# Squares between two feed-forward products: ScalarE's second activation in place of GpSimd's product

## The chip, the cores and the metric

The kernel runs on one core of a Trainium2 chip. The metric is the device time of one execution in microseconds (us); the time before is a median over three runs. The core has five engines that take instructions in the order in which they stand: TensorE (PE in the profile; its weight loads have a row of their own, PEld), VectorE (DVE), ScalarE (ACT), GpSimd (POOL) and SyncE (SP), which here issues nearly all DMAs.

## The reference, cut to what matters

A sequence of 1024 frames of 1024 channels runs through two layers. Each has a token mixer (RWKV-7 in the first layer, an S5 state-space layer with a gated projection in the second) and then a feed-forward block; a layer norm follows every one of the four. The change lies in the feed-forward block alone:

```
def sq_relu_mlp(x, w1, w2):
    return jnp.square(jax.nn.relu(x @ w1)) @ w2

h = layer_norm(DN_ALPHA * h + sq_relu_mlp(h, mlp_w1[i], mlp_w2[i]), ln_g[2*i+1], ln_b[2*i+1])
```

`w1` is 1024 x 4096 and `w2` 4096 x 1024, all in float32. The square of the rectified value stands between the two products.

## The kernel before

Channels lie on the 128 partitions and frames along a row. The frames are taken in two halves of 512, so a tile is 128 x 512: half A (`hA`, operands `oAh`, `oAl`) and half B (`hB`, `oBh`, `oBl`).

**Products in three parts.** A float32 operand is split into a high part of TensorE's own float32 kind and a remainder: `split` has ScalarE cast the high part (L152) and VectorE subtract it (L153). A product is then three matmuls (L198): high by high, high by low, low by high. Weights go the same way: SyncE brings 128 x 512 of them into `wraw`, ScalarE casts `whi`, VectorE makes `wlo`. `wraw` has two buffers, `whi` and `wlo` three each.

**A feed-forward block.** `blocks` gives two functions. `up(b)` makes two tiles of 128 hidden channels: 24 matmuls into a PSUM tile `d` (three buffers for the whole kernel), ScalarE's Relu of it into `rl` (L986), the square in place (L987), and the split into `qbuf` (L152, L153). `down(b)` multiplies these two tiles with `w2`, in eight groups of six matmuls, and VectorE adds each PSUM result into `hA` or `hB` (L1003). `up(b+1)` stands ahead of `down(b)`, so that a block's squares are wanted only a block later.

**Both halves at once.** In the second layer twelve of the sixteen blocks are done for both halves together by `both`, with seven half-size products (L1040) in place of eight. There `power` does Relu (L1046), square (L1047) and split, four times a block, into `qh` and `ql`.

Squares are 128 in all: 80 of L987 and 48 of L1047.

**What sets the order.** The code does not fix the order of the instructions. A scheduler puts them on the engines, by priorities that the kernel sets with `rank(...)`, by the buffers that are free, and by its own idea of what each instruction costs. So another engine or cost at one place can move the instructions around it on every engine.

**Where the blocks lie.** The first layer's blocks for half A run beside the last chunks of the RWKV recurrence (about 760 to 1005 us), beside the layer norm of half B and the building of the S5 tables (`s5_tables`, a chain of VectorE products, L1266 to L1268, with small TensorE products `pk` and `pb`; about 1040 to 1270 us). Those of half B run beside the layer norm and the S5 layer of half A (products L1310, L1317, L1331, L1383, L1391) and then alone, to about 1675 us. The second layer's blocks run from about 1950 us to the end.

**A layer norm** takes a sum (L870 to L876), `pm` (L878), subtraction (L880), squares on ScalarE (L884, L887), their sum on VectorE and GpSimd (L888), `pq` (L892), a power on GpSimd (L895), `pr` (L900), a product (L903) and scale and shift on ScalarE (L904).

Of the kernel before, what the change touches and what calls it, by code (L numbers as in the profile page):

```python
# [10 lines left out]
AF = mybir.ActivationFunctionType  # L11
# [61 lines left out]
def trunk(ctx, tc, A):  # L73
    nc = tc.nc
    V, S, G, PE, SP = nc.vector, nc.scalar, nc.gpsimd, nc.tensor, nc.sync
# [75 lines left out]
    def split(src, hi, lo, e=None):  # L151
        S.copy(hi, src)  # L152
        (e or V).tensor_sub(lo, src, hi.bitcast(F32))  # L153
# [12 lines left out]
    def wload(src, kt, n, key=None):  # L166

        step = 512 // n
        out = []
        for k0 in range(0, kt, step):  # L170
            kept = low.get((key, k0)) if key else None
            raw = wp.tile([128, step, n], F32, tag="wraw", name="wraw", bufs=2)
            SP.dma_start(raw, src[:, k0 : k0 + step])
            hi = wp.tile([128, step, n], F32R, tag="whi", name="whi")
            lo = wp.tile([128, step, n], F32R, tag="wlo", name="wlo")
            nw[0] += 1
            if kept is not None:
                SP.dma_start(lo.bitcast(F32).rearrange("p k n -> p (k n)"), kept)
                S.copy(hi, raw)
            else:  # L180
                split(raw, hi, lo, G if nw[0] % WLG[0] in WLG[1] and WLG[2] <= nw[0] < WLG[3] else V)
                if key:
                    low[key, k0] = dr.tile([128, 512], F32, name=f"low{len(low)}")
                    SP.dma_start(low[key, k0], lo.bitcast(F32).rearrange("p k n -> p (k n)"))
            out += [(hi[:, k], lo[:, k]) for k in range(step)]
        return out
# [35 lines left out]
    def dense(p, w, xs):  # L222
        n = len(xs)
        for k in range(n):
            mm3(p, w[k][0], w[k][1], xs[k][0], xs[k][1], k == 0, k == n - 1)
# [11 lines left out]
    def psd():  # L237
        return pd.tile([128, HT], F32, tag="d", name="d")
# [736 lines left out]
    def blocks(i, h, xo, qbuf):  # L975

        nw = 512 // KB2
        qs = {}

        def up(b):  # L980
            qs[b] = []
            for n in range(KB2):
                p = psd()
                dense(p, wload(A["mw1"][i, b * KB2 + n], KT, 128), xo)
                r = tp.tile([128, HT], F32, tag="ev", name="rl", bufs=EVB)
                S.activation(r, p, AF.Relu)  # L986
                G.tensor_mul(r, r, r)  # L987
                qt = qbuf[:, n + KB2 * (b % 2)]
                split(r, qt[:, 0], qt[:, 1])
                qs[b].append((qt[:, 0], qt[:, 1]))  # L990

        def down(b, first=False, cs=slice(0, HT)):
            for n2 in range(C // nw):
                w = wload(A["mw2"][i, b, n2], KB2, nw)
                for n in range(nw // 128):
                    p = psd()[:, cs]
                    dense(p, [(x[:, n * 128 : (n + 1) * 128], y[:, n * 128 : (n + 1) * 128]) for x, y in w],
                          [(x[:, cs], y[:, cs]) for x, y in qs[b]])
                    z = h[n2 * (nw // 128) + n][:, cs]
                    if first:  # L1000
                        V.scalar_tensor_tensor(z, z, ALPHA, p, op0=ALU.mult, op1=ALU.add)
                    else:
                        V.tensor_add(z, z, p)  # L1003

        return up, down

    def mlp(i, h, xo, qbuf):
# [10 lines left out]
    def both(i, hP, hQ, P, Q, tops, first):  # L1018

        nw = 512 // KB2  # L1020
        P1, P2, Q2 = P[0:4], P[4:8], Q[4:8]
        T1, T2, T3, T4 = tops
        qs = {}

        def raw(pool, tag, f, k0):
            t = pool.tile([128, 4, 128], F32, tag=tag, name="raw", bufs=2)
            SP.dma_start(t, A["mw1"][i, f][:, k0 : k0 + 4])
            return t

        def weights(t):  # L1030
            hi = wp.tile([128, 4, 128], F32R, tag="whi", name="whi")
            lo = wp.tile([128, 4, 128], F32R, tag="wlo", name="wlo")
            split(t, hi, lo)
            return hi, lo

        def product(p, t, xs, add=False):
            hi, lo = weights(t)
            for k in range(4):
                for j, (w, x) in enumerate(((hi, xs[k][0]), (hi, xs[k][1]), (lo, xs[k][0]))):
                    PE.matmul(p, w[:, k], x, start=not add and k + j == 0, stop=k == 3 and j == 2, skip_group_check=True)  # L1040

        def ev(name):
            return tp.tile([128, HT], F32, tag="ev", name=name, bufs=EVB)

        def power(dst, x):
            S.activation(dst, x, AF.Relu)  # L1046
            G.tensor_mul(dst, dst, dst)  # L1047
            qh, ql = (jp.tile([128, HT], F32R, tag=nm, name=nm, bufs=6) for nm in ("qh", "ql"))
            split(dst, qh, ql)
            return qh, ql  # L1050

        def up(b):
            f1, f2 = 2 * b, 2 * b + 1
            r11, r12 = raw(wp, "wraw", f1, 0), raw(wp, "wraw", f1, 4)
            r21, r22 = raw(tp, "la", f2, 0), raw(tp, "la", f2, 4)
            s1, s2 = (tp.tile([128, 4, 128], F32, tag="m", name=nm, bufs=2) for nm in ("s1", "s2"))
            G.tensor_add(s1, r21, r22)
            G.tensor_sub(s2, s1, r11)
            pa_ = psd()
            product(pa_, r11, P1)  # L1060
            m1 = ev("m1")
            S.copy(m1, pa_)
            pb_ = psd()
            product(pb_, s2, T2)
            V.tensor_add(m1, pb_, m1)
            product(pa_, r12, P2, True)
            r = ev("rl")
            c1 = power(r, pa_)
            G.tensor_sub(r21, r11, r21)
            pc_ = psd()  # L1070
            product(pc_, r21, T3)
            u3 = ev("u3")
            V.tensor_add(u3, pc_, m1)
            pd_ = psd()
            product(pd_, s1, T1)
            m5 = ev("m5")
            S.copy(m5, pd_)
            G.tensor_sub(s2, r12, s2)
            pe_ = psd()
            product(pe_, r22, T4)  # L1080
            G.tensor_add(m5, m5, u3)
            V.tensor_sub(u3, u3, pe_)
            product(pd_, s2, Q2, True)
            V.tensor_add(m1, pd_, m1)
            c2, c4, c3 = power(u3, u3), power(m5, m5), power(m1, m1)
            qs[b] = (c1, c2), (c3, c4)

        def down(b):
            for n2 in range(C // nw):
                w = wload(A["mw2"][i, b, n2], KB2, nw)  # L1090
                for n in range(nw // 128):
                    for h, q, fresh in ((hP, qs[b][0], b == first), (hQ, qs[b][1], False)):
                        p = psd()
                        dense(p, [(x[:, n * 128 : (n + 1) * 128], y[:, n * 128 : (n + 1) * 128]) for x, y in w], q)
                        z = h[n2 * (nw // 128) + n]
                        if fresh:
                            V.scalar_tensor_tensor(z, z, ALPHA, p, op0=ALU.mult, op1=ALU.add)
                        else:
                            V.tensor_add(z, z, p)

        return up, down
# [491 lines left out]
```

## Time and profile before

| | |
|---|---|
| time, median of 3 runs | 2673.59 us (2672.07 to 2679.01) |
| the profiled execution, its own time | 2674.25 us |
| its span, first to last instruction | 2672.5 us |
| mean granted TensorE clock | 0.960 |
| busy: PE, DVE, ACT, POOL | 2495.2, 1846.4, 1133.2, 629.8 us |
| L987, 80 squares on POOL | 90.8 us |
| L1047, 48 squares on POOL | 53.02 us |

A group's row in the profile has the line, the engine, the operation, what it writes and reads, the shapes and the count, then the busy time, the mean duration of one in ns, and the idle time of the engine just before these instructions with what ended it. A row of a table by stretches has each engine's busy time in the stretch with the number of its instructions, the granted TensorE clock (1.00 is full), the share of the DMA engines' time and what they moved. A row of waits names the waiting instruction, what ended the wait, the sum, the number and the longest.

### The profile page before, as it was taken

How to read it: one execution, taken by the hardware profiler on the slowest of the kernel's cores; microseconds unless marked ns; L12 is line 12 of the kernel's file. 1: busy time of each engine (PE TensorE's matmuls, PEld its weight loads, DVE VectorE, ACT ScalarE, POOL GpSimd, SP SyncE). 2: the span in 40 equal slices, each digit the busy share in tenths (PEclk: the TensorE clock that was granted, in tenths of full speed). 3: DMA queues.
4: the chain of work that ended last, by engine and by line, in shares of the span. 5: the costliest groups of instructions: out<-in, count | busy, mean ns of one | idle time of the engine just before them, and what ended most of it. 6: DMA issues, size and time to landing. Idle time of an engine off the chain costs nothing.

```text
span 2672.5 us, 43745 instructions
## 1 busy us (share of the span) xinstructions
PE 2495.2 (93%) x16624; PEld 2022.1 (76%) x16624; DVE 1846.4 (69%) x3271; ACT 1133.2 (42%) x2028; POOL 629.8 (24%) x532
## 2 busy tenths in 40 slices
PE   7899979989889999888899999998999999999996
PEld 5678757788667777766777888886777888888875
DVE  7367677487896868799785555775587656565576
ACT  7555665554444334245433333433453322323234
POOL 3121542342442222011100011200233313223111
PEclk9999889998889999999999999998999999999998
DMA  4765455663323324456465333264222111111133
GB/s 152 243 217 182 155 166 178 206 183 126 97 74 92 93 93 141 132 155 154 148 224 179 99 95 96 90 210 143 91 83 79 56 51 52 52 51 52 52 103 99
DMA packets 213074, 330.31 MB, mean 124 GB/s; under 512 B 20736, under 2 KB 85376, under 8 KB 212864
## 3 DMA queue, kind: packets, MB, share of 16 engines
q1 hardware_dynamic: 212864, 327.52, 39.3%
q8 instruction: 131, 2.15, 0.3%
q14 instruction: 79, 0.65, 0.1%
HBM read 260.28 MB, written 67.16 MB: 123 GB/s over the span
## 4 chain that ended last, share of the span: by engine, by line
PE 54%; DVE 11%; DMA 4%; issue 2%; ACT 1%; SPq 1%; POOL 1%; ACTq 0%; DVEq 0%; POOLq 0%
PE d L198 40%; PE d L1040 9%; DVE wlo L153 2%; DMA wraw<-in_mw_dram 2%; DMA yl<-s_y 1%; PE pu L1317 1%; DVE hA L1003 1%; PE pbu L1331 1%; DVE qbuf L153 0%; DVE hA L880 0%; ACT whi L152 0%; PE py L1383 0%; DMA s_y<-yg 0%; DVE tw L1267 0%; DVE ca L1266 0%
## 5 line engine op out<-in xcount | busy, mean ns | idle before, releaser
L152 ACT CAST whi<-wraw 128x512 fp32r<-128x512 f32 x524 | 324.3, 619 | 748.5 <-PE d L198 430.3
L153 DVE TENSOR_TENSOR wlo<-wraw,whi 128x512 fp32r<-128x512 f32 x524 | 409.1, 782 | 271.9 <-ACT whi L152 266.0
L198 PE MATMUL d<-qbuf,whi 128*128 128x512 f32 (+1 forms) x1344 | 414.5, 391 | 21.4 <-DVE hA L1003 13.7
L198 PE MATMUL d<-oAh,whi 128*128 128x512 f32 (+1 forms) x768 | 310.8, 412 | 14.2 <-ACT ev L428 9.3
L198 PE MATMUL d<-oAh,wlo 128*128 128x512 f32 (+1 forms) x768 | 309.4, 409 | 9.7 <-DVE wlo L153 6.3
L198 PE MATMUL d<-oAl,whi 128*128 128x512 f32 (+1 forms) x768 | 306.7, 403 | 8.2 <-DVE oAl L153 8.2
L198 PEld LDWEIGHTS d<-qbuf,whi 128*128 128x128 f32 x1344 | 248.5, 192 | 80.2 <-DVE hA L1003 15.8
L198 PE MATMUL d<-qbuf,wlo 128*128 128x512 f32 (+1 forms) x672 | 259.3, 388 | 6.5 <-DVE wlo L153 6.3
L987 POOL TENSOR_TENSOR rl<-rl 128x512 f32<-128x512 f32 x80 | 90.8, 1136 | 704.2 <-ACT rl L986 677.9
L198 PE MATMUL d<-oBh,whi 128*128 128x512 f32 x512 | 204.0, 400 | 13.5 <-ACT whi L152 10.4
L198 PE MATMUL d<-oBh,wlo 128*128 128x512 f32 x512 | 203.7, 399 | 8.1 <-DVE wlo L153 8.1
L198 PE MATMUL d<-oBl,whi 128*128 128x512 f32 x512 | 202.5, 396 | 0.0
L198 PEld LDWEIGHTS d<-oAh,whi 128*128 128x128 f32 (+1 forms) x768 | 147.3, 194 | 49.2 <-ACT ev L428 11.6
L198 PEld LDWEIGHTS d<-oAh,wlo 128*128 128x128 f32 (+1 forms) x768 | 147.2, 193 | 44.9 <-DVE wlo L153 8.5
L198 PEld LDWEIGHTS d<-oAl,whi 128*128 128x128 f32 (+1 forms) x768 | 147.8, 194 | 39.3 <-DVE oAl L153 10.1
L198 PEld LDWEIGHTS d<-qbuf,wlo 128*128 128x128 f32 x672 | 128.1, 191 | 35.0 <-DVE wlo L153 9.4
L198 PE MATMUL d<-qh,wlo 128*128 128x512 f32 x384 | 151.4, 394 | 0.0
L198 PE MATMUL d<-ql,whi 128*128 128x512 f32 x384 | 150.6, 392 | 0.0
L198 PE MATMUL d<-qh,whi 128*128 128x512 f32 x384 | 149.3, 389 | 0.0
L198 PEld LDWEIGHTS d<-oBh,whi 128*128 128x128 f32 x512 | 97.3, 191 | 37.8 <-ACT whi L152 12.4
L1003 DVE TENSOR_TENSOR hB<-hB,d 128x512 f32<-128x512 f32 (+1 forms) x168 | 104.4, 632 | 30.6 <-PE d L198 28.8
L198 PEld LDWEIGHTS d<-oBh,wlo 128*128 128x128 f32 x512 | 97.4, 190 | 31.7 <-DVE wlo L153 10.0
(455 smaller groups left out, 5175.1 us busy)
## 6 DMA issues: line engine op xcount, KB each, us to landing
wraw<-in_mw_dram SPq DMA_DIRECT2D x376, 256.0 KB, 2.7
wraw<-in_glu_dram SPq DMA_DIRECT2D x64, 256.0 KB, 2.7
low<-wlo SPq DMA_DIRECT2D x52, 256.0 KB, 2.8
wlo<-low SPq DMA_DIRECT2D x52, 256.0 KB, 3.8
raw<-in_mw_dram SPq DMA_DIRECT2D x48, 256.0 KB, 2.6
wraw<-in_wk_dram SPq DMA_DIRECT2D x32, 256.0 KB, 3.4
wraw<-in_wr_dram SPq DMA_DIRECT2D x32, 256.0 KB, 4.0
wraw<-in_wv_dram SPq DMA_DIRECT2D x32, 256.0 KB, 4.4
```

Source lines behind the costliest of these rows:

```text
L152: S.copy(hi, src)
L153: (e or V).tensor_sub(lo, src, hi.bitcast(F32))
L198: bulk.append((PE.matmul(p, w, x, **kw).ins, x.shape[-1]))
L987: G.tensor_mul(r, r, r)
L1003: V.tensor_add(z, z, p)
L1040: PE.matmul(p, w[:, k], x, start=not add and k + j == 0, stop=k == 3 and j == 2, skip_group_check=True)
L1317: PE.matmul(p[64 * (1 - e) : 64 * (1 - e) + 64, g], u1[:, j, g].rearrange("p s c -> p (s c)"), sel[:, e], start=True, stop=True)
L1331: PE.matmul(p[qs, ri, g2], tb[:, g2, ri, qs], u[:, 2 * g2 + par], start=True, stop=True)
```

## The change

Both squares are taken by ScalarE's Square activation in place of GpSimd's product of the tile with itself. What is computed, and the tiles it goes through, stay the same.

```
@@ up, in blocks
                 S.activation(r, p, AF.Relu)
-                G.tensor_mul(r, r, r)
+                S.activation(r, r, AF.Square)
                 qt = qbuf[:, n + KB2 * (b % 2)]
                 split(r, qt[:, 0], qt[:, 1])
@@ power, in both
             S.activation(dst, x, AF.Relu)
-            G.tensor_mul(dst, dst, dst)
+            S.activation(dst, dst, AF.Square)
             qh, ql = (jp.tile([128, HT], F32R, tag=nm, name=nm, bufs=6) for nm in ("qh", "ql"))
             split(dst, qh, ql)
```

The scheduler answers with another order on all engines between the last chunks of the recurrence and the first S5 layer, and with nearly the same one after it. The order is shown at three places.

GpSimd around the layer norm of half B and the S5 tables; `sq` are the norm's sums of squares, `rs` its power, `oBl` remainders of its result. Before:

```order
L871 TENSOR_TENSOR sa<-sa,hB 128x512
L1234 MEMSET kpad_12928 128x4x128
L1234 MEMSET kpad_12929 128x4x128
L987 TENSOR_TENSOR rl<-rl 128x512
L888 TENSOR_TENSOR sq_12052<-sq_12052,sq 128x512
L987 TENSOR_TENSOR rl<-rl 128x512
L888 TENSOR_TENSOR sq_12052<-sq_12052,sq 128x512 x2
L895 TENSOR_TENSOR rs<-rs,mhalf 128x4
L987 TENSOR_TENSOR rl<-rl 128x512
L153 TENSOR_TENSOR oBl<-hB,oBh 128x512
```

and now:

```order
L871 TENSOR_TENSOR sa<-sa,hB 128x512
L1234 MEMSET kpad_12928 128x4x128
L1234 MEMSET kpad_12929 128x4x128
L888 TENSOR_TENSOR sq_12052<-sq_12052,sq 128x512 x3
L895 TENSOR_TENSOR rs<-rs,mhalf 128x4
L153 TENSOR_TENSOR oBl<-hB,oBh 128x512 x3
```

The norm's instructions stand on GpSimd without squares of the feed-forward block between them.

ScalarE in the same stage, from one Relu of the feed-forward block to the norm's first squares; `bs` and `bp` belong to the S5 tables. Before:

```order
L986 ACTIVATE rl<-d 128x512
L1296 COPY bs<-pb_13000 128x512
L1261 COPY bp<-bb 128x8x16
L152 CAST qbuf<-rl 128x512
L152 CAST whi<-wraw 128x512
L884 ACTIVATE sq_12051<-hB 128x512
L884 ACTIVATE sq_12052<-hB 128x512
```

and now:

```order
L986 ACTIVATE rl<-d 128x512
L152 CAST whi<-wraw 128x512
L987 ACTIVATE rl<-rl 128x512
L152 CAST qbuf<-rl 128x512
L152 CAST whi<-wraw 128x512
L884 ACTIVATE sq_12051<-hB 128x512
L884 ACTIVATE sq_12052<-hB 128x512
```

One square (L987) stands now on ScalarE, ahead of the cast into `qbuf`, of a weight's cast and of the norm's squares.

TensorE where the S5 layer of half A begins; `pu` are its transposed inputs, made from `hA` and then, by way of ScalarE's copies into `u`, a second time. Now:

```order
L1310 MATMUL pu_13492<-ident,hA 128x128 x4
L1310 MATMUL pu_13498<-ident,hA 128x128 x4
L198 MATMUL d<-qbuf,whi 128x512 x2
L198 MATMUL d<-qbuf,wlo 128x512
L198 MATMUL d<-qbuf,whi 128x512 x2
L198 MATMUL d<-qbuf,wlo 128x512
L1317 MATMUL pu_13504<-sel,u_13491 64x64 x16
L1317 MATMUL pu_13563<-sel,u_13491 64x64 x16
```

and before, up to the same products:

```order
L1310 MATMUL pu_13492<-ident,hA 128x128 x4
L1310 MATMUL pu_13498<-ident,hA 128x128 x4
L198 MATMUL d<-qbuf,whi 128x512 x2
L198 MATMUL d<-qbuf,wlo 128x512
L198 MATMUL d<-qbuf,whi 128x512 x2
L198 MATMUL d<-qbuf,wlo 128x512
L198 MATMUL d<-qbuf,whi 128x512 x2
L198 MATMUL d<-qbuf,wlo 128x512
L198 MATMUL d<-qbuf,whi 128x512 x2
L198 MATMUL d<-qbuf,wlo 128x512
L198 MATMUL d<-qbuf,whi 128x512 x2
L198 MATMUL d<-qbuf,wlo 128x512
```

Before, 24 matmuls of the feed-forward block stand between the two steps (the listing has the first 15); now there are 6.

More of the change, by code (lines that the diff above doesn't have):

```diff
@@ L986, in up @@
                 S.activation(r, p, AF.Relu)
-                G.tensor_mul(r, r, r)
+                S.activation(r, r, AF.Square)
                 qt = qbuf[:, n + KB2 * (b % 2)]
@@ L1046, in power @@
             S.activation(dst, x, AF.Relu)
-            G.tensor_mul(dst, dst, dst)
+            S.activation(dst, dst, AF.Square)
             qh, ql = (jp.tile([128, HT], F32R, tag=nm, name=nm, bufs=6) for nm in ("qh", "ql"))
```

## The prediction

> **What bounds the kernel now.** First the page: the busy shares, and the chain of work that ended last.
>
> ```profile
> PE 2495.2 (93%) x16624; PEld 2022.1 (76%) x16624; DVE 1846.4 (69%) x3271; ACT 1133.2 (42%) x2028; POOL 629.8 (24%) x532
> PE 54%; DVE 11%; DMA 4%; issue 2%; ACT 1%; SPq 1%; POOL 1%; ACTq 0%; DVEq 0%; POOLq 0%
> ```
>
> TensorE sets the time. GpSimd, which loses work, and ScalarE, which gains it, each hold 1% of the chain. A share is a mean over stages, so I read the table by stretches next, cut where squares are taken (the first eight numbers' meaning: start and end, length, then PE, PEld, DVE, ACT, POOL).
>
> ```profile
> 804.00:1005.00 201.00, 200.98 (x1594) 160.51 (x1593) 141.10 (x260) 79.42 (x145) 43.65 (x38) 1.00 0.31 93
> 1005.00:1139.00 134.00, 120.92 (x583) 97.05 (x580) 104.90 (x241) 41.22 (x72) 20.23 (x16) 0.94 0.47 143
> 1139.00:1273.00 134.00, 113.44 (x687) 87.29 (x686) 122.20 (x177) 63.44 (x120) 19.71 (x14) 0.97 0.62 152
> 1273.00:1474.00 201.00, 190.55 (x1599) 153.89 (x1599) 144.63 (x262) 77.59 (x134) 21.57 (x19) 0.98 0.55 182
> 1474.00:1675.00 201.00, 201.00 (x881) 165.28 (x880) 107.56 (x165) 64.17 (x110) 19.53 (x19) 1.00 0.32 96
> 1943.00:2077.00 134.00, 125.21 (x534) 100.99 (x534) 105.65 (x146) 64.68 (x112) 44.62 (x32) 0.97 0.26 81
> 2077.00:2500.00 423.00, 423.00 (x1847) 346.65 (x1846) 251.24 (x357) 127.55 (x219) 112.64 (x94) 1.00 0.16 50
> ```
>
> In 804 to 1005, 1474 to 1675 and 2077 to 2500 TensorE has no gap and its full clock, and the other engines have room: there no square can be worth anything. Between 1005 and 1474 it idles 13.1 + 20.6 + 10.4 = 44.1 us, and 8.8 us in 1943 to 2077; there the granted clock is below 1 as well. In 1139 to 1273 VectorE is busy 122.2 of 134 us: that stretch is VectorE's. Third, what ended TensorE's waits over the whole span (sum, times, longest):
>
> ```profile
> PE d L198 <- DVE wlo L153: 22.7, 18, 3.6
> PE d L198 <- ACT whi L152: 20.5, 7, 7.9
> PE d L198 <- DVE hA L1003: 13.7, 10, 3.6
> PE d L198 <- ACT rl L986: 2.9, 2, 2.2
> ```
>
> It waits for weights (a cast or a remainder) and for PSUM tiles that VectorE has yet to add; for a square or the `qbuf` behind it, never. So the change acts only through what it does to VectorE's and ScalarE's queues in the stretches with gaps.
>
> **What it removes.** The squares on GpSimd, and who stood behind them:
>
> ```profile
> L987 POOL TENSOR_TENSOR rl<-rl 128x512 f32<-128x512 f32 x80 | 90.8, 1136 | 704.2 <-ACT rl L986 677.9
> L1047 POOL TENSOR_TENSOR m<-m x24: 1039/1041/1575, 2069.4 to 2502.6; 128x512 f32<-128x512 f32 x24
> L152 ACT CAST qbuf<-rl 128x512 fp32r<-128x512 f32 x80 | 49.6, 620 | 70.1 <-POOL rl L987 69.7
>   ACT whi L152: 13.5, 11
> ```
>
> The last row is from the list of those who waited for L1047. ScalarE loses 69.7 + 13.5 = 83.2 us of waiting for GpSimd. A single case shows the size, and a bad one:
>
> ```profile
> 815.51 1.04 POOL L987 TENSOR_TENSOR rl<-rl 128x512 f32<-128x512 f32 x1 [5.67 <-ACT rl L986]
> 816.04 1.05 DVE L153 TENSOR_TENSOR wlo<-wraw,whi 128x512 fp32r<-128x512 f32 x1 [1.05 <-ACT whi L152]
> 1158.79 2.86 POOL L987 TENSOR_TENSOR rl<-rl 128x512 f32<-128x512 f32 x1 [23.98 <-ACT rl L986]
> 1161.69 0.62 ACT L152 CAST qbuf<-rl 128x512 fp32r<-128x512 f32 x1 [2.30 <-POOL rl L987]
> ```
>
> At 1158.79 VectorE is in a dense run and the square takes 2.86 us instead of 1.04; ScalarE stands for 2.30 us.
>
> **What it adds.** 128 Squares on ScalarE. The norm takes such squares already, of the same shape, between Relus:
>
> ```profile
> L887 ACT ACTIVATE sq<-hA 128x512 f32<-128x512 f32 x24 | 14.5, 626 | 6.1 <-DVE sq L888 3.5 <-POOL sq L888 2.6
> L986 ACT ACTIVATE rl<-d 128x512 f32<-128x512 f32 x80 | 47.4, 592 | 5.1 <-PE d L198 4.9
> ```
>
> 128 x 0.626 = 80.1 us busy, against 83.2 us of waiting gone: ScalarE's queue is occupied as long as before. What stands behind a square is a `qbuf` cast and then weight casts. What hides the addition is the idle time ahead of these:
>
> ```profile
> L152 ACT CAST whi<-wraw 128x512 fp32r<-128x512 f32 x524 | 324.3, 619 | 748.5 <-PE d L198 430.3 <-DMA wraw<-in_mw_dram 133.0 <-DMA wraw<-in_wo_dram 36.6
> ```
>
> 748.5 / 524 = 1.43 us each, mostly waiting for a free weight buffer (TensorE) or a transfer. I cost it at nothing; with that cover gone it would be 0.626 us a square, in the stretches with gaps alone (see the rivals).
>
> **What VectorE gains.** The `wlo` at 816.04 ran 0.51 us beside a square (815.51 + 1.04 - 816.04) and took 1.05 us. The rows for its kind, for one of the same shape in the quiet stretch, and for a VectorE instruction that reads PSUM:
>
> ```profile
> L153 DVE TENSOR_TENSOR wlo<-wraw,whi 128x512 fp32r<-128x512 f32 x524 | 409.1, 782 | 271.9 <-ACT whi L152 266.0
> L153 DVE TENSOR_TENSOR wlo<-s,whi 128x512 fp32r<-128x512 f32 x36 | 24.6, 683 | 2.5 <-ACT whi L152 2.5
> L1003 DVE TENSOR_TENSOR hA<-hA,d 128x512 f32<-128x512 f32 x144 | 97.1, 681 | 25.6 <-PE d L198 24.3
> ```
>
> Against the quiet 0.683 the case lost 1.05 - 0.68 = 0.37 us. Bounds for one square's cost to VectorE: none (the neighbour is an L1003, 0.681 on the mean, or VectorE idles) and the whole 1.04 us of the square. I take 0.37, the one pair that the rows show. The Trainium skill, "SBUF — State Buffer", section "Who interferes with whom", has it harsher: a VectorE instruction with two SBUF inputs and a GpSimd instruction that reads SBUF exclude each other, and whichever starts first holds the pair for all its time. By that rule alone 1.04 us a square would be near; the trace agrees in kind (782 against 683 ns on the mean, and PSUM readers at 681), while the pair above lost only 0.37 us.
>
> Squares per stretch (GpSimd's busy time in L987 and their number):
>
> ```profile
> 1005.00:1139.00 134.00, 7.01 (x6) 0.94 0.47 143
> 1139.00:1273.00 134.00, 8.57 (x6) 0.97 0.62 152
> 1273.00:1474.00 201.00, 14.20 (x13) 0.98 0.55 182
> 1943.00:2077.00 134.00, 10.25 (x8) 0.97 0.26 81
> 1943.00:2077.00 134.00, 5.08 (x4) 0.97 0.26 81
> ```
>
> (The last row is L1047.) In 1139 to 1273 VectorE is the limit and I count all six: 6 x 0.37 = 2.2 us. In the other three stretches VectorE is busy 72 to 79%, so I count a third, as a choice: 31 x 0.37 / 3 = 3.8 us. Together -6.0 us; the bounds are 0 and (6 + 31 / 3) x 1.04 = -17.0 us.
>
> **What the new order costs.** Nothing of the computation moves between stages, but its interleaving does. Where the first S5 layer begins, TensorE now has 6 matmuls of cover in place of 24 between the transposes (L1310) and the products (L1317) that need ScalarE's two copies:
>
> ```profile
> 1313.55 1.11 PE L1310 MATMUL pu<-ident,hA 128*128 128x128 f32 x8
> 1317.02 0.58 ACT L1311 COPY u<-pu 128x512 f32<-128x512 f32 x1
> ```
>
> The second copy ends at 1317.60, and six matmuls, at the pace of the stretch without gaps (423.00 / 1847 = 0.229 us each), end 1.4 us after 1314.66, at about 1316.0. If ScalarE is as late as before, TensorE waits 1.6 us; if it makes the copies as soon as the transposes are there, nothing. I take +1, nearer the row. For the reordering as a whole I have no row; as ends I take the largest single wait above, 7.9 us, given away once or saved once, and nothing as the value.
>
> **The sum.** 2674.25 (the profiled execution's own time, span 2672.5 and 1.75 around it) - 6.0 + 1.0 + 0 = 2669.25. That execution lies 0.66 us above the median of 2673.59, so in terms of the median 2668.6; I forecast **2669 us**. Its own range is 6 us either way, 2663 to 2675: the relief may be missed whole, or the order may bring as much again.
>
> **The rivals.**
>
> *VectorE is held for the whole square.* Then the relief is 17.0 us in place of 6.0: 2674.25 - 17.0 + 1.0 - 0.66 = 2657.6, 2658 us. For it: L987's own 2.86 us beside a dense run, and the mean of 1136 ns against 1.04 for one alone, which shows each side losing. Against it: the pair at 816, and that in 1005 to 1139 and 1273 to 1474 most of TensorE's waits are for weights that ScalarE or a transfer brings late. The rule of the Trainium skill on "SBUF — State Buffer" cited above would give this.
>
> *Hidden after all.* If the gaps are ended by transfers and the casts behind them, VectorE's relief changes nothing: 2674 us. For it: 7.9 us of the 20.5 us for `whi` is a single wait; against it: 22.7 us for `wlo`, 13.7 for L1003.
>
> *ScalarE comes late (slower).* In 1005 to 1474, 25 squares stand in a queue with the norm's squares, the tables' copies and weight casts. If the idle time ahead of the next weight cast is under 0.626 us there, each square makes `whi`, then `wlo`, then TensorE late by that: 25 x 0.626 = 15.7 us, 2674.25 + 15.7 - 6.0 + 1.0 - 0.66 = 2684 us. It decides from about ten squares without cover (10 x 0.626 > 6.0). For it: one wait of 2.2 us for a Relu (L986) shows ScalarE late once already, and the waiting for GpSimd that goes was no loss where the next weight had not landed. Against it: 63.4 of 134 us busy in the densest stretch, and the waiting that goes.
>
> **How the numbers follow.** A measurement here tells about 0.3% from no change, 8 us: faster means under 2665.6, slower over 2681.6. Chances: the forecast 0.48, whole-square relief 0.20, hidden 0.12, ScalarE late 0.20. Faster: 0.19 of the second case and three tenths of the forecast's, 0.34. Slower: three quarters of the last, and 0.04 from a worse order, 0.19. The rest, 0.47, is no change that can be told. The range runs from the one rival to the other, 2657 to 2684; it leaves out less than 2 in 10 beyond each of their middles.
>
> **What would show it.** Right: `qbuf` casts no longer wait for GpSimd; 128 Squares near 0.63 us; ScalarE's busy time near 1213 us; GpSimd's near 486; `wlo` on the mean under 782 ns; the three stretches without gaps as long as before; the gain, where there is one, between 1005 and 1474. Wrong: TensorE's waits for `whi` or L986 grown by more than 6 us between 1005 and 1474 (ScalarE late), or VectorE's busy time down by over 40 us and the idle time of that stretch by over 12 (whole squares), or a change in the length of a stretch without gaps.

## The result, and the profile after

The changed kernel takes 2655.4 us (median of 6 runs, 2652.6 to 2658.8) against 2673.8 us for the kernel before beside it: ratio 0.993, 95% interval 0.9918 to 0.9942. Measured on two more chips it came to 0.9916 and 0.9925. So the change brings 18 to 22 us; 5 were forecast, and the time lies just below the range that was given. The profiled execution takes 2656.89 us, its span is 2655.1.

First the page of the changed kernel, busy shares and the chain of work that ended last:

```profile
PE 2491.6 (94%) x16624; PEld 2019.2 (76%) x16624; DVE 1809.0 (68%) x3271; ACT 1212.6 (46%) x2156; POOL 494.6 (19%) x404
PE 64%; DVE 16%; DMA 9%; ACT 4%; issue 4%; POOL 1%; SPq 1%; ACTq 0%; DVEq 0%; POOLq 0%
```

ScalarE has become busier by 79.4 us, as forecast, and VectorE, whose instructions have not changed, less busy by 37.4 us. The groups of instructions that the change touches, in the changed kernel:

```profile
L987 ACT ACTIVATE rl<-rl 128x512 f32<-128x512 f32 x80 | 50.5, 632 | 1.9
L152 ACT CAST qbuf<-rl 128x512 fp32r<-128x512 f32 x80 | 49.6, 620 | 2.0
L152 ACT CAST whi<-wraw 128x512 fp32r<-128x512 f32 x524 | 324.5, 619 | 725.4 <-PE d L198 468.7 <-DMA wraw<-in_mw_dram 126.6 <-DMA wraw<-in_wo_dram 25.5
L153 DVE TENSOR_TENSOR wlo<-wraw,whi 128x512 fp32r<-128x512 f32 x524 | 394.3, 754 | 258.9 <-ACT whi L152 252.9 <-PE d L198 2.5 <-DMA s_k<-ev 1.4
```

What ended TensorE's waits over its whole span (sum, times, longest):

```profile
PE d L198 <- ACT whi L152: 19.6, 8, 7.7
PE d L198 <- DVE wlo L153: 14.6, 12, 2.9
PE d L198 <- DVE hA L1003: 12.0, 10, 3.1
PE d L198 <- ACT rl L986: 3.4, 3, 1.2
```

The casts into `qbuf` wait 2.0 us in all where they waited 70.1; `wlo` takes 754 ns in place of 782. TensorE waits 14.6 us for `wlo` where it waited 22.7; for ScalarE (`whi`, `rl`) it waits as before. The table by stretches, at the limits used in the prediction:

```profile
804.00:1005.00 201.00, 201.00 (x1561) 161.31 (x1560) 140.25 (x273) 88.31 (x158) 24.51 (x21) 1.00 0.32 95
1005.00:1139.00 134.00, 122.14 (x630) 97.13 (x630) 102.69 (x243) 47.25 (x82) 15.63 (x12) 0.98 0.46 138
1139.00:1273.00 134.00, 122.70 (x726) 95.52 (x726) 125.14 (x190) 68.58 (x129) 17.78 (x9) 0.97 0.65 167
1273.00:1474.00 201.00, 190.41 (x1600) 154.27 (x1599) 141.03 (x257) 87.92 (x150) 5.15 (x4) 0.97 0.56 180
1474.00:1675.00 201.00, 201.00 (x881) 165.20 (x880) 110.55 (x167) 76.88 (x127) 0.00 (x0) 1.00 0.33 96
2077.00:2500.00 423.00, 423.00 (x1846) 346.42 (x1845) 235.67 (x360) 148.53 (x252) 68.19 (x49) 1.00 0.17 50
```

The stretches without gaps stay without gaps. Where TensorE idled 20.6 us (1139 to 1273) it now idles 11.3, and does more matmuls in the same time (726 for 687). Fixed limits cut the two programs at slightly different work, so from here on a stretch is bounded by two TensorE instructions: from the 57th transposition of L790 to the 49th of L1401, 1023 to 1425 us before. It holds the end of the recurrence, the S5 tables, both layer norms and the start of the S5 layer, with 20 squares. Its row in the table by stretches, before:

```profile
1023.40:1424.80 401.40, 360.09 (x2509) 286.44 (x2507) 330.48 (x614) 158.86 (x284) 55.87 (x43) 0.96 0.57 168
```

and in the changed kernel, measured a third time (e15):

```profile
1028.70:1414.60 385.90, 357.22 (x2506) 284.76 (x2504) 319.61 (x614) 170.20 (x303) 36.08 (x23) 0.97 0.59 175
```

The same work takes 385.9 us in place of 401.4; TensorE's idle time falls from 41.3 to 28.7 us, VectorE's busy time from 330.5 to 319.6. The other two profiles of the changed kernel, the first one and e7, have 387.5 and 391.5 us here, so one pair of profiles leaves some 6 us open.

### The profile page after: what moved, and what is told of

The parts are those of the page before. It is cut to its first block, busy times and chain, and to the rows that moved or that the text cites. A ratio compares the mean times of both kernels' runs of the same rounds, so it can differ in the third digit from the quotient of the medians.

```text
span 2655.1 us, 43705 instructions
## 1 busy us (share of the span) xinstructions
PE 2491.6 (94%) x16624; PEld 2019.2 (76%) x16624; DVE 1809.0 (68%) x3271; ACT 1212.6 (46%) x2156; POOL 494.6 (19%) x404
## 4 chain that ended last, share of the span: by engine, by line
PE 64%; DVE 16%; DMA 9%; ACT 4%; issue 4%; POOL 1%; SPq 1%; ACTq 0%; DVEq 0%; POOLq 0%
PE d L198 48%; PE d L1040 9%; DVE wlo L153 3%; DMA wraw<-in_mw_dram 2%; DVE oAl L153 1%; ACT whi L152 1%; DMA yl<-s_y 1%; DMA lda<-s_a 1%; DVE xh L653 1%; PE pA L607 1%; DVE x L651 1%; DMA s_y<-yg 1%; DMA wraw<-in_wr_dram 1%; DVE KB L577 1%; PE pu L1317 1%
## 5 line engine op out<-in xcount | busy, mean ns | idle before, releaser
L153 DVE TENSOR_TENSOR wlo<-wraw,whi 128x512 fp32r<-128x512 f32 x524 | 394.3, 754 | 258.9 <-ACT whi L152 252.9
L198 PE MATMUL d<-oBh,whi 128*128 128x512 f32 x512 | 206.1, 405 | 14.8 <-ACT whi L152 10.0
L198 PEld LDWEIGHTS d<-qbuf,wlo 128*128 128x128 f32 x672 | 127.1, 189 | 29.7 <-DVE wlo L153 4.6
L1003 DVE TENSOR_TENSOR hA<-hA,d 128x512 f32<-128x512 f32 x144 | 97.6, 685 | 26.6 <-PE d L198 25.5
```

The source lines that it names most:

```text
L198: bulk.append((PE.matmul(p, w, x, **kw).ins, x.shape[-1]))
```

## Experiments: which part of the change

Three things changed at once: GpSimd no longer works beside VectorE, ScalarE no longer waits for GpSimd but takes the squares itself, and every engine has another order. Kernels marked "order of ..." have each engine's instructions tied into the order of the kernel named, and only what the diff shows differs. Each is compared with the kernel before on its own chip.

| kernel | order of | squares on | added | ratio, 95% interval |
|---|---|---|---|---|
| e1 / e10 | before | ScalarE | | 0.9938 [0.9914, 0.9963] / 0.9943 [0.9926, 0.996] |
| e2 | after | GpSimd | | 0.9957 [0.994, 0.9975] |
| e3 | after | ScalarE | idle products, 400 columns | 0.9933 [0.9909, 0.9956] |
| e4 / e12 | its own | blocks on ScalarE, power on GpSimd | | 0.9899 [0.987, 0.9928] / 0.9921 [0.9906, 0.9937] |
| e8 | its own | power on ScalarE, blocks on GpSimd | | 0.9994 [0.9979, 1.0008] |
| e6 / e11 | before | ScalarE | idle products, 400 columns | 0.9974 [0.9963, 0.9984] / 0.9979 [0.9965, 0.9994] |
| e17 | before | ScalarE | idle products, 512 columns | 1.0013 [0.9998, 1.0027] |
| e18 | before | GpSimd, not waited for | | 1.0016 [1.0001, 1.0031] |
| e5 | before | ScalarE | pass that the cast waits for | 1.0019 [1.0006, 1.0032] |
| e9 | after | ScalarE | the same | 1.0043 [1.0028, 1.0059] |
| e13 | after | ScalarE | the same, 27 squares | 0.9991 [0.9981, 1.0001] |
| e14 | after | ScalarE | the same, the other 101 | 0.9983 [0.9973, 0.9993] |
| e16 | after | ScalarE | the same, 128 columns | 0.9938 [0.9918, 0.9958] |
| e7 / e15 | | the changed kernel again | | 0.9916 [0.9902, 0.993] / 0.9925 [0.9913, 0.9937] |

e1 to e4 and, later, e17 and e18 ran on one chip by the record, e5 to e8 on a second, e9 to e12 on a third, e13 to e16 on a fourth.

**The squares without the new order (e1), the new order without the squares (e2).** e1 is the change, e2 the kernel before, each with a chain of dependencies along every engine (`seq` is the other kernel's order):

```
+    for n in seq:
+        i = have.get(f"I-{n}")
...
+        if e in last:
+            tc.add_manual_dep(i, last[e], mybir.DependencyInfo(
+                mybir.DependencyClass.NoSync, mybir.DependencyReason.DATA), reason="order")
+        last[e] = i.name
```

> Squares on ScalarE, but every engine's instructions held in the order of the kernel before, each square standing on ScalarE where it stood among all instructions before. If the gain of 18 us is the new order: 2670 to 2676 us. If it is the relief of VectorE and ScalarE (no GpSimd product beside VectorE's, no wait for GpSimd): 2655 to 2660 us. Half and half: about 2665 us.

> Squares on GpSimd, every engine's instructions held in the order of the changed kernel, each square on GpSimd where it stood among all instructions. If the gain is the new order: 2653 to 2658 us. If it is the relief: 2670 us or more, since ScalarE now has a cast of qbuf waiting for GpSimd in an order that was made for none.

Measured 0.9938 and 0.9957. Most of the gain needs no new order. The new order alone is worth 0.4% too, but the two don't add up: together they give 0.9916 to 0.993. Both shorten the same stretch: from 401.4 us before to 395.3 (e1) and 388.6 (e10), and to 392.7 (e2).

**Blocks or power (e4, e8).** One of the two lines is changed and the other left on GpSimd:

```
@@ e4: up, in blocks
-                G.tensor_mul(r, r, r)
+                S.activation(r, r, AF.Square)
@@ e8: power, in both
-            G.tensor_mul(dst, dst, dst)
+            S.activation(dst, dst, AF.Square)
```

> Only the 80 squares of blocks on ScalarE, the 48 of power stay on GpSimd. TensorE has no gap where power runs, so by every theory the whole gain stays: 2654 to 2658 us. If the 48 matter after all, by their relief of VectorE around 1950 to 2080 us: up to 3 us more, 2658 to 2661 us.

> Only the 48 squares of power on ScalarE, the 80 of blocks stay on GpSimd. TensorE has no gap where power runs: 2672 to 2676 us where before takes 2674. Since the kernel with blocks alone took 0.990 of before against 0.993 for both, power on ScalarE may cost: then 2676 to 2684 us.

The power's 48 squares are worth nothing (0.9994), the blocks' 80 the whole. That agrees with the stretch 2077 to 2500, where TensorE has no gap with either. e4 looked better than the whole change; it was run again:

> Only the 80 squares of the blocks on ScalarE, the power's 48 on GpSimd as before, a second time. The first time it was 0.9899 where the whole change is 0.993. If leaving the power's squares on GpSimd is really better by 8 us: 0.989 to 0.991 here, below the changed kernel's interval [0.9918, 0.9942]. If the power's squares are worth nothing either way, as the run with these alone moved says (0.9994): 0.991 to 0.994.

0.9921 this time: it can't be told from the changed kernel.

## Experiments: VectorE's neighbour, or ScalarE's wait

**Idle products (e6, e11, and e3 in the new order).** Behind each Square GpSimd multiplies the tile by itself into a tile that nobody reads; nothing is left out of the computation.

```
                 S.activation(r, r, AF.Square)
+                G.tensor_mul(junk, r[:, 0:400], r[:, 0:400])
...
             S.activation(dst, dst, AF.Square)
+            G.tensor_mul(junk, dst[:, 0:400], dst[:, 0:400])
```

> The changed kernel in its own order, plus, after each of the 128 Squares, a GpSimd product of the square's first 400 columns with themselves into a tile that nobody reads (this one is extra work, nothing of the computation is left out). GpSimd then runs beside VectorE about as much as before (400/512 of it), and nothing waits for it. If VectorE's relief from GpSimd is the cause: most of 18 us x 0.78 = 14 us comes back, 2666 to 2670 us. If it is the order, or ScalarE's waits for GpSimd: 2654 to 2658 us.

> Squares on ScalarE in the order of the kernel before, plus the idle GpSimd product of 400 columns after each Square that nobody waits for (extra work). It puts back GpSimd beside VectorE without ScalarE's wait. If the wait is the cause: as e1_act_oldorder, 2655 to 2661 us on a chip where before takes 2674. If VectorE's relief is the cause: 2668 us or more.

> The Squares on ScalarE in the order of the kernel before, a second time, now on one chip with the next two kernels (the first time it was 0.9938 on a chip where the kernels with GpSimd's idle work had not run). If that value stands, 0.992 to 0.996. If the two chips differ and the presence of GpSimd's work was never worth 0.36%, it comes out at 0.996 to 0.998, as the run with the idle products did.

> The old order, Squares on ScalarE and an idle product of 400 columns on GpSimd behind each, a second time. If the presence beside VectorE costs about 10 us in that order: 0.996 to 0.999, 0.003 to 0.004 above the run without it on this chip. If it costs nothing: within 0.001 of that run.

In the order of before, GpSimd's presence takes back 0.36% (0.9943 to 0.9979, one chip). In the new order the ratio shows nothing that can be told (0.9933 against 0.9916 to 0.993, on other chips; the intervals leave up to 0.3%), though VectorE is as much busier, 1835.1 against 1809.0 us. By e3's own expectation, which had 2666 to 2670 us for VectorE's relief, the 2657.4 us measured speak against it. But the trace of e3 does show a cost. From TensorE's 13517th matmul to its 14064th, with 12 squares, the row of the changed kernel:

```profile
1929.99:2063.91 133.92, 126.62 (x549) 102.40 (x547) 101.07 (x148) 72.64 (x127) 28.54 (x21) 0.99 0.26 81
```

and of e3:

```profile
1928.68:2065.91 137.23, 128.31 (x549) 103.32 (x547) 104.47 (x148) 72.67 (x127) 40.56 (x33) 0.98 0.27 79
```

The changed kernel's other two profiles have 132.5 and 132.4 us here. e2, which has all squares on GpSimd in this order and ScalarE's wait with them, has 137.2 us, and its ratio, 0.9957, is 0.3% above the changed kernel's. So in the new order GpSimd's products aren't free either, in this stretch at least.

**The whole presence, and the wait alone (e17, e18).** 400 columns are not 512, and what was left of the gain could be ScalarE's wait or the missing columns. e17 has all 512; its idle result goes as bfloat16. e18 is the kernel before with the squares into the idle tile, so that the casts read the Relu's output: the squaring is left out of what is computed, GpSimd works as before, and ScalarE takes no Square and doesn't wait for GpSimd ahead of `qbuf`. (13.4 us of waiting for GpSimd stay, ahead of weight casts between 2060 and 2492 us, nearly all where TensorE has no gap.)

```
@@ e17
                 S.activation(r, r, AF.Square)
+                G.tensor_mul(junk, r, r)
@@ e18
                 S.activation(r, p, AF.Relu)
-                G.tensor_mul(r, r, r)
+                G.tensor_mul(junk, r, r)
```

> The order of before, Squares on ScalarE, and behind each an idle product on GpSimd over all 512 columns (its result goes as bfloat16 into a tile that nobody reads). With 400 columns it was 0.9974 and 0.9979. If the whole gain in the old order (0.994) is GpSimd's presence, 0.9990 to 1.0005. If presence goes with the columns and the rest is ScalarE's wait that is gone: 0.36% x 512 / 400 above 0.994, 0.9983 to 0.9990. If 112 columns more change nothing: 0.997 to 0.998.

> The order of before, with GpSimd's products of all 512 columns as they were, but into a tile that nobody reads (as bfloat16); the casts take the Relu's output itself. So the squaring is left out of what is computed, GpSimd's presence stays, ScalarE neither waits for GpSimd nor takes a Square. The ratio is the worth of ScalarE's wait alone. If the wait is worth nothing, as the prediction had it: 0.999 to 1.001. If the 83.2 us of it cost 12 us (0.45%, as the whole pass with its wait did against idle products): 0.994 to 0.997. If it costs the 0.2% left over and the Squares' own time has taken as much again, as 128 x 0.63 us against 83.2 us would have it: 0.996 to 0.998.

All three have the order of before. The page's busy line of e10, without squares or idle products on GpSimd:

```profile
PE 2491.0 (94%) x16624; PEld 2018.3 (76%) x16624; DVE 1816.2 (69%) x3271; ACT 1212.5 (46%) x2156; POOL 486.2 (18%) x404
```

The same line of e17:

```profile
PE 2502.4 (94%) x16624; PEld 2025.9 (76%) x16624; DVE 1851.5 (69%) x3271; ACT 1212.3 (45%) x2156; POOL 632.7 (24%) x532
```

and of e18:

```profile
PE 2500.0 (94%) x16624; PEld 2025.2 (76%) x16624; DVE 1848.6 (69%) x3271; ACT 1134.5 (43%) x2028; POOL 628.0 (24%) x532
```

The group of the casts into `qbuf` of e18:

```profile
L153 ACT CAST qbuf<-rl 128x512 fp32r<-128x512 f32 x80 | 49.5, 619 | 1.6
```

e17: with the presence whole, the gain in that order is gone, 1.0013. e18: with ScalarE's wait gone (1.6 us left of 70.1) and no Square in its place, nothing is gained, 1.0016. So in the order of before the whole 0.70% between e10 and e17, 18.7 us, is GpSimd's work. Their intervals, on two chips, leave 13 to 25 us; on one chip, e1 and e17 differ by 0.75%. It acts beside VectorE, and not by making GpSimd's other results late: in e10 and e1 GpSimd ended 77.4 and 70.8 us of ScalarE's waits, 13.7 and 15.7 of VectorE's and 4.6 and 4.5 of TensorE's, in e17 74.9, 14.8 and 4.6. The common stretch shows it. Its row in e10:

```profile
1023.80:1412.40 388.60, 357.02 (x2508) 284.48 (x2507) 319.59 (x614) 170.61 (x304) 32.02 (x23) 0.97 0.58 174
```

and in e17:

```profile
1031.10:1430.70 399.60, 361.38 (x2509) 286.20 (x2508) 332.86 (x614) 171.21 (x304) 58.50 (x43) 0.96 0.57 169
```

20 idle products make VectorE's 614 instructions 13.3 us longer and the stretch 11.0 us longer. In 6.6 us of these TensorE idles more; in the other 4.4 it is busy longer with the same work, at a granted clock of 0.96 in place of 0.97. Against e1, the kernel of e10 on another chip, the products cost only 9.7 us of VectorE and 4.3 us of the stretch (e1 has 323.21 and 395.30 us). So here are the lengths between the same TensorE matmuls in all five kernels, named by their times before (us):

| stretch before | squares | before | e17 | e18 | e10 | e1 |
|---|---|---|---|---|---|---|
| 1023 to 1139 | 6 | 115.4 | 116.1 | 114.2 | 111.0 | 112.1 |
| 1139 to 1273 | 6 | 134.4 | 131.8 | 130.4 | 127.5 | 129.4 |
| 1273 to 1425 | 8 | 151.6 | 151.6 | 152.8 | 150.1 | 153.7 |
| 1943 to 2077 | 12 | 133.9 | 134.1 | 135.1 | 130.7 | 130.7 |

With GpSimd's products (the first three kernels) the first and the last of these stretches are longer than without by 2 to 5 us; the second is longer too, less evenly; in the third nothing can be told. That is some 11 of the 18.7 us (e17 against the mean of e10 and e1); the rest these profiles don't place. One pair from the timelines, a table product of VectorE. Before, beside the square of 2.86 us that the prediction quotes:

```profile
1160.79 1.81 DVE L1268 TENSOR_TENSOR bp<-bp,tw 128x896 f32<-128x896 f32 x1
```

and in e17, where no GpSimd product is near it:

```profile
1158.98 1.08 DVE L1271 TENSOR_TENSOR bp<-bp,tw 128x896 f32<-128x896 f32 x1
```

Here one square cost VectorE 0.73 us.

**The wait put back (e5).** After each Square GpSimd multiplies the tile by 1.0 in place, and the cast must wait for it, in the order of before:

```
                 S.activation(r, r, AF.Square)
+                G.tensor_scalar(r, r, 1.0, None, op0=ALU.mult)
...
             S.activation(dst, dst, AF.Square)
+            G.tensor_scalar(dst, dst, 1.0, None, op0=ALU.mult)
```

> Squares on ScalarE in the order of the kernel before (as in e1_act_oldorder), and after each Square a GpSimd pass over the same tile, times 1.0, before the cast may read it (extra work, nothing left out). It puts back ScalarE's wait for GpSimd and GpSimd's presence beside VectorE, and keeps the 80 us of Squares. If the wait is what the change took away: the gain is gone, 2672 to 2685 us on a chip where before takes 2674. If only the squares' place mattered (order, VectorE's relief from two-input products): 2656 to 2662 us.

1.0019: the gain is gone. Taken alone I read this as the worth of the wait. e17 and e18 correct it: the wait of before is free, and e5's was longer, because a Square stands in front of it and the pass takes 1.6 us on the mean. Its casts into `qbuf` wait 113.6 us where they waited 70.1:

```profile
L152 ACT CAST qbuf<-rl 128x512 fp32r<-128x512 f32 x80 | 49.7, 621 | 113.6 <-POOL rl L988 113.6
```

**How long a wait is free (e9, e13, e14, e16).** The same pass in the new order: after all Squares, after 27 taken between 1005 and 1474 us, after the others, and over 128 columns only.

> The changed kernel with every engine held in its own order, and one addition: after each of the 128 Squares on ScalarE GpSimd multiplies the same tile by 1.0 in place, and the cast that reads it next waits for that, as it waited for GpSimd's square before. In the old order putting GpSimd and the wait back took the whole gain (1.0019 of the time of before). If ScalarE's waiting is what the change removes, whatever the order: the gain goes here too, 0.997 to 1.002, 2666 to 2679 us where the kernel before takes 2673. If the new order has given ScalarE enough distance between a square and its cast, as the 0.9957 of the new order with GpSimd's squares suggests, the ratio stays between 0.993 and 0.997: the same as that run, plus the 5 us that the Squares themselves cost. If neither matters in the new order, 0.990 to 0.993.

> The changed kernel in its own order, with GpSimd's pass of 1.0 over the tile, for which the cast waits, after 27 Squares of the blocks alone (numbers 19 to 45, taken between 1005 and 1474 us, where TensorE has gaps). All 128 of them had cost 1.2% (1.0043 against about 0.992). If the wait costs only where TensorE has gaps, as the prediction had it for the whole change: nearly all of it here, ratio 1.000 to 1.004. If each wait costs the same wherever it stands, 27/128 of 32 us, 7 us: 0.994 to 0.996. By the stages of the two single profiles, half: 0.997 to 0.999.

> The same pass and wait after the other 101 Squares alone (before 1005 us, after 1474 us, and all of the power's). If the wait costs only where TensorE has gaps: as the changed kernel, 0.991 to 0.994. If each costs the same: 25 us, 1.000 to 1.003. By the stages of the two single profiles, half: 0.997 to 0.999.

> The changed kernel in its own order, with a pass over 128 of 512 columns after each of the 128 Squares, for which the cast waits. By columns, a quarter of the time on GpSimd, with the hop to GpSimd and back as before. If the cost follows the time that ScalarE stands (or GpSimd works beside VectorE): about a third of the 32 us, 0.995 to 0.997. If the hop itself is most of it (two semaphores and the break of the queue): 0.998 to 1.002. If nothing happens below a threshold, because the queue had slack for short waits: 0.991 to 0.994.

> The changed kernel, a third time, on the chip of the other three: 0.991 to 0.994 by the two measurements so far.

> The changed kernel again beside the others on one chip: 0.993 of before, 2655 us where before takes 2674.

The group of the casts into `qbuf`, between 1005 and 1474 us alone, before:

```profile
L152 ACT CAST qbuf<-rl 128x512 fp32r<-128x512 f32 x25 | 15.5, 619 | 17.8 <-POOL rl L987 17.6
```

in e16:

```profile
L152 ACT CAST qbuf<-rl 128x512 fp32r<-128x512 f32 x26 | 16.1, 620 | 18.1 <-POOL rl L988 18.1
```

and in e13:

```profile
L154 ACT CAST qbuf<-rl 128x512 fp32r<-128x512 f32 x25 | 15.5, 619 | 39.5 <-POOL rl L991 39.4
```

The row of the common stretch in e16:

```profile
1015.30:1407.50 392.20, 359.65 (x2505) 286.36 (x2504) 321.90 (x613) 169.47 (x302) 51.23 (x43) 0.97 0.58 172
```

and in e13:

```profile
1025.50:1427.90 402.40, 361.36 (x2505) 287.19 (x2503) 324.81 (x613) 169.62 (x302) 68.33 (x43) 0.96 0.57 168
```

With 18.1 us of waiting and about 16 us of Squares (26 x 0.63), e16 costs 0.13% against e15, and the intervals overlap. With 39.5 us and 16 us, e13 costs 0.66%, 17.6 us, 0.65 us for each of 27 squares. VectorE is hardly busier there than in e15 (324.8 against 319.6 us in the stretch, 1813.2 against 1807.4 in all), so most of this loss is not VectorE's; what else the pass adds is ScalarE's wait. The other 101 cost 0.58% together, 0.15 us each (e14), and the two add up to e9's. e14's loss can't be put down to the wait alone: its VectorE is 29.7 us busier than e15's (1837.1 against 1807.4). It also lengthens the stretch 2077 to 2500, without gaps before and in the changed kernel, from 423.1 to 427.7 us. ScalarE's cover between 1005 and 1474 us is finite: it bore some 34 us there, and not 55.

## Why the prediction was wrong

**What bounds the kernel, and where.** Right: TensorE with its gaps between 1005 and 1474 us, VectorE as the engine that is late there; the stretches of 201, 201 and 423 us without gaps stayed so.

**ScalarE's squares at nothing.** Right, and now shown: the swap of 83.2 us of waiting for 80.1 us of Squares moves nothing. The wait ahead of `qbuf` alone is worth nothing (e18 against the kernel before), and neither are the Squares: e17 has them, e18 doesn't, both with GpSimd's products and on one chip, 1.0013 and 1.0016. The rival *ScalarE comes late* fell: TensorE's waits for `whi` and `rl` did not grow. Its mechanism exists, at 55 us of waiting and Squares in place of 34 (e13 and e16).

**What VectorE gains, -6.0 us. This is the step that failed**, by its size. The kind was right: GpSimd's squares lengthen VectorE's instructions, and TensorE waits for these. It measured 18.7 us (13 to 25) in the order of before. Two choices made it small. The first weighs more: of the squares outside 1139 to 1273 only a third was counted, because VectorE is busy 72 to 79% there. For the 12 squares ahead of 2077 us that gave 12 x 0.37 / 3 = 1.5 us, and e17 against e10 and e1 shows 3.4; for the six between 1005 and 1139 it gave 0.7 us, and they show 4 to 5. A stretch's share says nothing of the moments at which TensorE waits for VectorE. Without the third, 37 x 0.37 = 13.7 us, inside the interval. The second choice is the 0.37 us a square, from one pair: over the common stretch before had VectorE 330.48 us busy and e10 319.59, with 20 squares 0.54 us each; with e1 in e10's place 0.36. All 37 squares at these prices are 13 to 20 us. That is a sum after the fact, since between 1273 and 1425 us no loss shows.

**The rival *VectorE is held for the whole square*, 2658 us**, came nearest in time, but not by its own price. VectorE did not lose the whole 1.04 us per square: it lost 0.36 to 0.54 us in the common stretch, and over the run 37.4 / 128 = 0.29 us. Nor did its signs appear: VectorE lost 37.4 us, not over 40, and TensorE's idle time fell by 9.3 us between 1139 and 1273 and by 10.3 between 1005 and 1474, not by over 12. Its 17.0 us hit by luck, because 1.04 us on a third of the squares is near 0.54 us on all. The Trainium skill, "SBUF — State Buffer", section "Who interferes with whom", says that a VectorE instruction with two SBUF inputs and a GpSimd instruction that reads SBUF exclude each other, and for a whole instruction. The runs agree in kind (a VectorE product of 1.08 us took 1.81 us, and the GpSimd square beside it 2.86 in place of 1.04), while the mean stays at half the square's length or less.

**The new order, +1.0 and 0.** At the entrance of the S5 layer the size was right, the wait another. The products L1317 don't wait longer for the copies. List of what ended their waits, after:

```profile
  ACT u L1311: 0.4, 1
```

Before had the same 0.4 us. But right behind the transposes TensorE now stands for a PSUM tile that VectorE has yet to read:

```profile
1311.25 0.73 PE L198 MATMUL d<-qbuf,whi 128*128 128x512 f32 x2 [1.08 <-DVE hB L1001]
```

The two other profiles of the changed kernel have the same 1.1 us, and before has no gap there. The copies, which come 2.5 us after the transposes (1312.62 against 1310.17; before 2.9), hide behind it. The order as a whole is worth 1 to 3 thousandths beyond the squares (0.9943 for e10 against 0.9916 to 0.993), some 3 to 7 us and inside the 7.9 us allowed; the intervals overlap, so less can't be excluded.

**The range** reached down to 2657 us because the VectorE term had been bounded at 17.0 us. That bound itself kept the factor of a third. With all 37 squares whole it would have been 38.5 us.

**What stays open.** In the order of before 400 columns of idle work cost 0.36% and 512 columns 0.70%, more than in proportion by the medians; the intervals don't exclude proportion. Nor do they tell 0.36% there from 0.09% in the new order (e3 against the mean of the changed kernel's three ratios), so whether the new order hides part of the busier VectorE is not shown; idle products of 512 columns were not tried in it. And about half of the difference between the profiles of e10 and e17 is TensorE's busy time, 2491.0 against 2502.4 us for the same 16624 matmuls. The granted clock is lower in some of the stretches with gaps; no run separates it from the gaps.

## What to carry to other kernels

When work leaves an engine that shares something with the engine that is late, price it by the whole busy time that the late engine loses in the stretches with gaps, not by one pair and not scaled down by its mean share. Which of these stretches pay, only a run tells. A wait for another engine cost nothing here as long as the waiting queue had idle time behind it: swapping it for work of the same length was free, twice the wait on top of that work was not. To learn which of two causes paid, put each back alone with the order of instructions held.

## What was unexpected

- A wait put back by an extra pass misled, since it brought a longer wait than the one removed: e5 lost as much with a VectorE that is hardly busier as e17 with a ScalarE that doesn't wait (1.0019 and 1.0013).
- In the common stretch a pass of one operand on GpSimd disturbed VectorE less than a product: 20 passes made VectorE 5.2 us busier (e13, 324.81, against e15, 319.61), 20 products 13.3 us (e17 against e10), though a pass takes 1.5 us and more and a product 1.1. It isn't so everywhere: between 2077 and 2500 us passes made VectorE 28 us busier in e14 (261.9 against e15's 233.6) and hardly in e5 (242.0 against e10's 240.3), by the same TensorE matmuls. e5's page, in the order of before, has VectorE nearly as little busy in all as e10 (1816.2):

```profile
PE 2496.2 (93%) x16624; PEld 2017.6 (76%) x16624; DVE 1819.5 (68%) x3271; ACT 1209.4 (45%) x2156; POOL 687.8 (26%) x532
```

- Single profiles vary by stage: the first stage, which ends at 251.6 us before and has the same instructions in the same order in all kernels, ends between 244.4 (e16) and 257.7 us (e8). A change of 20 us can be placed by profiles only where several of them agree.
